# Moving quarter-array products of the recurrence beside others of their form in a two-layer decoder trunk

## The chip, the cores and the metric

The kernel runs on one core of a Trainium2 chip, as one program. The metric is the device time of one execution in microseconds (us). Lower is better. The engines are named as the profile names them: PE (TensorE, matrix products), PEld (its weight loads), DVE (VectorE), ACT (ScalarE), POOL (GpSimd) and SP (SyncE, which issues the DMAs).

## What is computed

Two layers, each with a parallel mix of heads and an MLP, on 512 positions of width 1024 in float32:

```python
for l in range(DEPTH):                       # 2
    h = rms_norm(x, norm_mix_g[l])
    proj = h @ w_in[l]                       # 1024 -> 26 groups of 128 columns
    p_att, p_conv, p_rwkv = jnp.split(proj, ...)
    o_att  = diff_attention(q, k, v, ...)    # 6 heads, two softmaxes each, causal
    o_conv = short_conv(...)
    o_rwkv = rwkv7_time_mix(p_rwkv, ...)     # 6 heads, a recurrence over 512 steps
    x = x + concat(o_att, o_conv, o_rwkv) @ w_out[l]
    h = rms_norm(x, norm_mlp_g[l])
    x = x + square(relu(h @ w_mlp_up[l])) @ w_mlp_down[l]
return rms_norm(x, final_norm_g)

# the recurrence in rwkv7_time_mix, for each head (state 64 x 64):
sa    = state @ (-kk_t)
state = state * w_t + sa (kk_t * a_t)^T + v_t k_t^T
y_t   = state @ r_t
```

## The kernel before

Large products (`pj` for the input projection, `po` for the output, `up`, `dn` and others for the MLP) are done in three passes of a split of both factors into a high and a low part; each pass is a 128x512 product on the whole array of PE. `raw` is a weight tile as it lands, `whi` and `wlo` its parts, `ahim` and `alom` those of the activations.

In the mix part of a layer other work is woven between these passes. The recurrence is done in chunks of 64 positions, two heads at a time: a *chain* t (0, 1, 2) for each pair of heads, written as `rwkv_pair(t)`, and the inverse that it needs, `rwkv_inverse(t)`. Their products are 64x64 blocks, so each uses a quarter of the array (64 rows by 64 columns of it) and four run on the quarters in turn. Groups that matter here, by their names in the profile: `pg` (the Gram products, two calls of `gram`, each into two banks of PSUM), `pbv` (16 products from `kq` and `vt`; ACT copies the result into `ab`), and in the inverse `px` and `py` (16 products each; ACT copies `px` into `rt`, which `py` needs), then `pz` and `pzz` on 32x32 blocks. `phsk` is a small product on columns of ones; DVE reads it into `rk`.

Attention (`att_pair`) is done row block by row block: `sc` (scores, two per block) on PE, a masked minimum `pp`/`mx` on DVE, two exponentials on ACT, three operations on DVE that end in `pp`, its transpose `ptt` on PE, a copy `pT` on ACT, and after four blocks the product `po<-v,pT`. `sc` and `ptt` share two banks.

What the order is, is written out by hand. Each of these functions is a generator that issues one instruction, or one group of products, and yields. `ORDER[l]` is a string with one letter for each step of a generator, and a count: `m` is the next product of the large ones, `R`, `S`, `T` a step of `rwkv_pair(0)`, `(1)`, `(2)`, `r`, `s`, `t` one of `rwkv_inverse`, `A`, `B`, `C` one of `att_pair`. `drive` goes through the string:

```python
    for run in order.split():
        for _ in range(int(run[1:] or 1)):
            if next(work[run[0]], True) is None:
                raise RuntimeError("a step before what it needs: " + run)
```

Each engine then does its instructions in that order, and waits on semaphores for what they need. `SLOTS[l]` deals buffers: for each tile in the order of its making a digit says which of the tag's buffers it takes. `ps/rp` deals the four PSUM banks that the recurrence's products rotate through; a product that takes a bank waits for the last reader of what lay there before.

Counted from 0, step 26 of a `rwkv_pair` is the first half of its Gram products, step 57 is `pbv`, steps 58 and 59 are the two copies on ACT from `pbv` into `ab`, step 10 is the first operation of DVE on `phsk`. Step 43 of a `rwkv_inverse` is `px`, 44 and 45 are the copies into `rt`, 46 is `py`.

Of the kernel before, what the change touches and what calls it, by code (L numbers as in the profile page):

```python
# [22 lines left out]
S = 512  # L23
# [3 lines left out]
C = 64  # L27
# [29 lines left out]
      "xyxyyxxxyyxxyyxyxxyxyyxyyyyyyxxxyyyxyxyyyyyyyxxxxxyyyyyyyyyyxyxyxxxxyyxxyy")  # L57

ORDER = (
# [43 lines left out]

SLOTS = (
         "cp/rk 010 "
         "cp/ro 010 "
         "cp/rr 10 "
         "cp/rsx 01201201 "
         "cp/ry 010 "
         "cp/ys 010 "  # L110
         "dp/dkhi 010 "
         "dp/dklo 010 "
         "dp/dm 010 "
         "dp/dn 010 "
# [18 lines left out]
         "mp/ty 010101010 "  # L133
         "ps/at 101010101010101010101010101010101010101010101010101010101010101010101010101010101010 "
         "ps/mm 01011101010001010101010101010101010101010 "
         "ps/rp 01233303103210321031230123012301230123231021302130213203131203102310202130123012301230123012301230101320312 "
         "wp/raw 01201201210210210210210210210210210210210210210210210210210210210210210210 "
         "wp/sq 101011010101010 "
         "wp/whi 01201201201201201201201201201201201201201201201201201201201201201201 "
# [29 lines left out]
         "mp/ty 010101010 "  # L169
         "ps/at 010101010101010101010101010101010101010101010101010101010101010101010101010101010101 "  # L170
         "ps/mm 01010100101010101010110101010101010101010101 "
         "ps/rp 10321032103210321023102310231023102021301230123012301230130231203131023012302130120312031203210303120132 "
         "wp/raw 12012012012012010210210210210210210210210210210210210210210210210210210210 "
         "wp/sq 101010101 "
         "wp/whi 01201201201201201201201201201201201201201201201201201201201201201201201201 "
# [1455 lines left out]
```

## Time and profile before

| what | us |
|---|---|
| time, median of 3 runs | 1241.3 |
| lowest, highest of the runs | 1240.41, 1241.66 |
| the profiled execution: time | 1239.57 |
| the profiled execution: span | 1237.8 |

The profile shows one execution. Its page gives busy times of each engine and the chain of work that ended last; the timeline lists instructions of an engine by their start, with their duration, and x32 is the number of records in the row (a float32 product of 64x64 makes two). All times in the text below are microseconds from the start of the span. The mix part of layer 0 lies at the start of the span up to about 250, that of layer 1 between about 620 and 870.

### The profile page before, as it was taken

The numbers are of one execution on the slowest core, as the hardware profiler recorded it, in microseconds if no ns is written. First come the engines' busy times: TensorE is split into PE (matmuls) and PEld (weight loads), VectorE is DVE, ScalarE is ACT, GpSimd is POOL, SyncE is SP. The second block draws the span as 40 slices with busy tenths as digits, with TensorE's granted clock in tenths as the row PEclk, the third lists the DMA queues.
The fourth block names the chain that finished last, engine by engine and source line by source line (L and its number), as shares of the span: only waits on it lengthen the run. The fifth ranks groups of instructions, "written<-read, shape, count | busy, mean of one in ns | idle before, by whom it ended". The sixth has DMA issues, their size and how long they took to land.

```text
span 1237.8 us, 25529 instructions
## 1 busy us (share of the span) xinstructions
PE 1226.2 (99%) x9716; PEld 1055.3 (85%) x9716; DVE 932.3 (75%) x1804; ACT 692.3 (56%) x1462; POOL 350.2 (28%) x449
## 2 busy tenths in 40 slices
PE   9999999999999999999999999999999999999997
PEld 6788788888999898989888887888889999999987
DVE  6787888869987676765666777887799867676753
ACT  6785655648455454544465657464675545454542
POOL 1263637331121111120035455464202211111111
PEclk9999999999999999999999999999999999999999
DMA  6523334142433333321235244232433333323121
GB/s 217 164 87 100 106 95 111 53 153 86 136 103 98 107 95 103 98 90 44 68 102 168 76 119 119 87 90 70 154 109 121 106 101 102 103 96 109 52 69 68
DMA packets 84698, 127.94 MB, mean 103 GB/s; under 512 B 21472, under 2 KB 25568, under 8 KB 84576
## 3 DMA queue, kind: packets, MB, share of 16 engines
q1 hardware_dynamic: 83568, 125.64, 33.0%
q8 instruction: 76, 1.25, 0.4%
q10 hardware_dynamic: 1008, 0.68, 0.2%
q14 instruction: 46, 0.38, 0.1%
HBM read 117.11 MB, written 9.18 MB: 102 GB/s over the span
## 4 chain that ended last, share of the span: by engine, by line
PE 94%; ACT 2%; DVE 2%; POOL 1%; DMA 1%; issue 1%; ACTq 0%; POOLq 0%; DVEq 0%
PE dn L282 25%; PE pj L282 21%; PE pa L282 13%; PE po L282 8%; PE pb L282 7%; PE dnF L282 4%; PE pc L282 3%; PE up L282 3%; PE sc L282 1%; PE ptt L287 1%; PE pg L282 1%; PE pyy L282 1%; DMA raw<-wts 1%; PE pzw L282 1%; PE pst L282 1%
## 5 line engine op out<-in xcount | busy, mean ns | idle before, releaser
L1394 POOL TENSOR_TENSOR ml<-m,mh 128x512 fp32r<-128x512 f32 x56 | 91.1, 1645 | 496.2 <-ACT mh L1393 337.6
L282 PE MATMUL dn<-mh,whi 128*128 128x512 f32 x448 | 175.5, 392 | 0.0
L282 PE MATMUL dn<-mh,wlo 128*128 128x512 f32 x448 | 175.2, 391 | 0.0
L282 PE MATMUL dn<-ml,whi 128*128 128x512 f32 x448 | 175.0, 391 | 0.0
L683 POOL TENSOR_TENSOR wlo<-raw,whi 128x512 fp32r<-128x512 f32 x84 | 111.5, 1328 | 206.0 <-ACT whi L671 170.6
L344 ACT CAST whi<-raw 128x512 fp32r<-128x512 f32 x126 | 77.9, 619 | 157.2 <-PE dn L282 147.7
L282 PE MATMUL pj<-ahim,whi 128*128 128x512 f32 x392 | 156.9, 400 | 0.4 <-DVE vf L1280 0.4
L282 PE MATMUL pj<-ahim,wlo 128*128 128x512 f32 x392 | 156.4, 399 | 0.0
L282 PE MATMUL pj<-alom,whi 128*128 128x512 f32 x392 | 156.0, 398 | 0.0
L1540 DVE TENSOR_TENSOR x<-dn,x 128x512 f32<-128x512 f32 x108 | 74.5, 690 | 88.7 <-PE dn L282 88.6
L671 ACT CAST whi<-raw 128x512 fp32r<-128x512 f32 x142 | 87.7, 617 | 78.0 <-PE pj L282 28.8
L1463 ACT CAST shi_p<-s 128x512 fp32r<-128x512 f32 x112 | 69.5, 621 | 78.5 <-PE pa L282 59.4
L345 DVE TENSOR_TENSOR wlo<-raw,whi 128x512 fp32r<-128x512 f32 x126 | 97.8, 778 | 7.1 <-ACT whi L344 6.8
L282 PEld LDWEIGHTS dn<-mh,wlo 128*128 128x128 f32 x448 | 84.2, 188 | 18.6
L282 PEld LDWEIGHTS dn<-ml,whi 128*128 128x128 f32 x448 | 84.2, 188 | 17.2
L282 PEld LDWEIGHTS dn<-mh,whi 128*128 128x128 f32 x448 | 84.1, 188 | 17.3
L282 PE MATMUL pa<-thi,shi_p 128*128 128x256 f32 x336 | 95.2, 283 | 0.0
L282 PE MATMUL pa<-tlo,shi_p 128*128 128x256 f32 x336 | 94.9, 282 | 0.0
L282 PE MATMUL pa<-thi,slo_p 128*128 128x256 f32 x336 | 94.1, 280 | 0.0
L1464 DVE TENSOR_TENSOR slo_p<-s,shi_p 128x512 fp32r<-128x512 f32 x112 | 77.7, 696 | 21.6 <-ACT shi_p L1463 18.8
L282 PEld LDWEIGHTS pj<-ahim,whi 128*128 128x128 f32 x392 | 73.9, 188 | 14.1 <-issue 0.8
L282 PEld LDWEIGHTS pj<-alom,whi 128*128 128x128 f32 x392 | 73.9, 188 | 14.0 <-issue 0.5
(417 smaller groups left out, 3248.6 us busy)
## 6 DMA issues: line engine op xcount, KB each, us to landing
raw<-wts SPq DMA_DIRECT2D x389, 256.0 KB, 2.6
qs<-dqhi SPq DMA_DIRECT2D x24, 128.0 KB, 3.3
ks<-dkhi SPq DMA_DIRECT2D x24, 128.0 KB, 3.6
x<-xT SPq DMA_DIRECT2D x8, 256.0 KB, 4.5
dqhi<-qhi SPq DMA_DIRECT2D x6, 256.0 KB, 3.5
dqlo<-qlo SPq DMA_DIRECT2D x6, 256.0 KB, 3.4
dkhi<-khi SPq DMA_DIRECT2D x6, 256.0 KB, 3.0
dklo<-klo SPq DMA_DIRECT2D x6, 256.0 KB, 3.5
```

The costliest lines, as they stand in the source:

```text
L282: ins = nc.tensor.matmul(*a, **k)
L287: ins = nc.tensor.transpose(*a, **k)
L344: act.copy(hi[:, :n], raw[:, :n])
L345: (pool if a and lean[0] else dve).tensor_tensor(lo[:, :n], raw[:, :n], hi[:, :n].bitcast(F32), ALU.subtract)
L671: yield act.copy(hi[:, k0:k1], raw[:, k0:k1])
L683: yield eng.tensor_tensor(lo[:, k0:k1], raw[:, k0:k1], hi[:, k0:k1].bitcast(F32), ALU.subtract)
L1394: (dve if i < 4 else pool).tensor_tensor(lo, m, hi.bitcast(F32), ALU.subtract)
L1463: act.copy(hi, src)
L1464: dve.tensor_tensor(lo, src, hi.bitcast(F32), ALU.subtract)
L1540: dve.tensor_tensor(x[j], pt, x[j], ALU.add)
```

## The change

Only the two tables are changed; what each step does is as before. Five groups of products move, which are numbered here for later:

1. layer 0, chain 0: `pbv` goes from between a `ptt` and a `po` to right behind chain 0's `px`, 17 us later; its two ACT copies go behind the two copies into `rt`.
2. layer 0, chain 1: `pbv` goes from behind a `po` to right behind chain 1's `px`, 2 us later. The ACT copies stay.
3. layer 1, chain 0: `pbv` goes from between two `pj` to right behind chain 0's `px`, 15 us later; the ACT copies as in 1.
4. layer 1, chain 1: `pbv` goes from between two `sc` to right behind chain 1's `py`, 13 us later; the ACT copies with it.
5. layer 1, chain 2: the first half of the Gram products goes from ahead of a `ptt` to right behind it, where the second half stands.

In layer 1 also step 10 of chain 2 (DVE on `phsk`) goes from behind chain 1's work on `py` to ahead of it. The banks of `ps/rp` are dealt anew for both layers: 58 of 107 digits differ in layer 0 and 54 of 104 in layer 1.

Pieces of the two tables (the strings are otherwise the same, but broken into lines at other places):

```diff
-  ... A2 r R3 m3 r A R r B3 r A R2 A h w r2 m2 ...
+  ... A2 r R3 m3 r A r B3 r A2 h w r2 m2 ...
-  ... y A2 m4 A r3 d m4 h S2 ...
+  ... y A2 m4 A r R r2 R2 d m4 h S2 ...
...
-  "ps/rp 10321032103210321023102310231023102021301230123012301230130231203131023012302130120312031203210303120132 "
+  "ps/rp 10321032103210321032103210321032103031201320132103210132320132013232103120312031021302021302130202310321 "
```

The first two pairs are move 1: `R` is taken out at the top (step 57, and below it `R2`, steps 58 and 59) and put behind `r` (step 43) and `r2` (44 and 45).

The instructions of PE at the old place of move 3, before:

```order
L282 MATMUL pj1_19_8499<-ahim1_6_7883,whi117_4_8455 128x512
L282 MATMUL pbv1_0_0_8594<-vt1_0_8389,kq1_0_8307 64x64 x2
L282 MATMUL pbv1_0_1_8595<-vt1_0_8389,kq1_0_8307 64x64 x2
...
L282 MATMUL pj1_19_8499<-alom1_6_7884,whi117_4_8455 128x512
L282 MATMUL pj1_19_8499<-ahim1_6_7883,wlo117_4_8465 128x512
L287 MATMUL ptt1_0_0_0_8622<-cst_77,pp1_0_0_0_0_8568 128x128
```

and now (a name is that of the tile with its layer, chain and numbers of making; line numbers are one higher):

```order
L283 MATMUL pj1_19_8499<-ahim1_6_7883,whi117_4_8455 128x512
L283 MATMUL pj1_19_8499<-alom1_6_7884,whi117_4_8455 128x512
L283 MATMUL pj1_19_8499<-ahim1_6_7883,wlo117_4_8465 128x512
L288 MATMUL ptt1_0_0_0_8602<-cst_77,pp1_0_0_0_0_8568 128x128
L283 MATMUL pj1_19_8499<-ahim1_7_7917,whi117_4_8455 128x512
```

Sixteen products less lie ahead of the transpose. At the new place of move 3, ACT before:

```order
L1180 COPY rt1_0_8817<-px1_0_0_8799 128x4x64
L1180 COPY rt1_0_8817<-px1_0_1_8800 128x4x64
L671 CAST whi102_0_8830<-raw102_0_8712 128x512
L1335 COPY pT1_0_0_8628<-ptt1_0_0_3_8820 128x512
L801 ACTIVATE dr1_1_8882<-pr1_1_8852,drv1_100 128x512
```

and now:

```order
L1181 COPY rt1_0_8815<-px1_0_0_8779 128x4x64
L1181 COPY rt1_0_8815<-px1_0_1_8780 128x4x64
L1025 COPY ab1_0_8387<-pbv1_0_0_8797 128x4x64
L1025 COPY ab1_0_8387<-pbv1_0_1_8798 128x4x64
L672 CAST whi102_0_8830<-raw102_0_8692 128x512
L1336 COPY pT1_0_0_8608<-ptt1_0_0_3_8820 128x512
```

The two copies stand ahead of a cast and of the attention's copy. DVE in layer 1 where `py` of chain 1 is read, before:

```order
L802 SCALAR_TENSOR_TENSOR zr2_1_9768<-pr2_1_9853,prm1_67,dr2_1_9885 128x512
L1188 TENSOR_TENSOR x16_1_1_9839<-py1_1_0_9920,x16_1_1_9839 128x4x64
L1188 TENSOR_TENSOR x16_1_1_9839<-py1_1_1_9921,x16_1_1_9839 128x4x64
L1190 STREAM_TRANSPOSE yj1_1_9948<-x16_1_1_9839 128x512
L909 TENSOR_SCALAR rk1_2_9973<-phsk1_2_9908 128x8
```

and now:

```order
L803 SCALAR_TENSOR_TENSOR zr2_1_9748<-pr2_1_9833,prm1_67,dr2_1_9865 128x512
L910 TENSOR_SCALAR rk1_2_9897<-phsk1_2_9888 128x8
L1189 TENSOR_TENSOR x16_1_1_9819<-py1_1_0_9902,x16_1_1_9819 128x4x64
L1189 TENSOR_TENSOR x16_1_1_9819<-py1_1_1_9903,x16_1_1_9819 128x4x64
L1191 STREAM_TRANSPOSE yj1_1_9950<-x16_1_1_9819 128x512
```

The read of `phsk` into `rk` stands ahead of the reads of `py`, whose second half now takes the bank of `phsk`.

More of the change, by code (lines that the diff above doesn't have):

```diff
@@ L135 @@
          "ps/mm 01011101010001010101010101010101010101010 "
-         "ps/rp 01233303103210321031230123012301230123231021302130213203131203102310202130123012301230123012301230101320312 "
+         "ps/rp 01233303103210321031203120312031203120201321032103210230123012301230101320312031203123012301320132020312301 "
          "wp/raw 01201201210210210210210210210210210210210210210210210210210210210210210210 "
```

87 rows, old and new, of the table ORDER are left out of this document.

## The prediction

> **What bounds the kernel now.** I read the page first (busy shares, chain of waits), then the timeline of TensorE (PE) around each of the five places that lose or gain quarter products, then the timelines of VectorE (DVE), ScalarE (ACT) and GpSimd (POOL) at the same times for what becomes ready when.
>
> ```profile
> span 1237.8 us, 25529 instructions
> PE 1226.2 (99%) x9716; PEld 1055.3 (85%) x9716; DVE 932.3 (75%) x1804; ACT 692.3 (56%) x1462; POOL 350.2 (28%) x449
> PE 94%; ACT 2%; DVE 2%; POOL 1%; DMA 1%; issue 1%; ACTq 0%; POOLq 0%; DVEq 0%
> ```
>
> PE is busy for 99% of the span and is 94% of the chain that ended last. So every nanosecond taken from PE would count, if PE were never late for a reason of its own. But ends of matmuls are modelled and overlap, so a short wait of PE does not show as idle time. I therefore use distances between starts, and compare them with the end of whatever the next product needs.
>
> **What a crossing into quarters costs.** The timeline of PE where chain 0 of layer 1 has its `pbv` (time of start, duration, what):
>
> ```profile
> 678.56 0.39 PE L282 MATMUL pj<-ahim,wlo 128*128 128x512 f32 x1
> 678.79 0.39 PE L282 MATMUL pj<-ahim,whi 128*128 128x512 f32 x1
> 679.11 0.69 PE L282 MATMUL pbv<-vt,kq 64*64 64x64 f32 x32
> 679.74 0.50 PE L282 MATMUL pj<-alom,whi 128*128 128x512 f32 x1
> 680.08 0.40 PE L282 MATMUL pj<-ahim,wlo 128*128 128x512 f32 x1
> 680.33 0.33 PE L287 MATMUL ptt<-cst,pp 128*128 128x128 f32 x1
> ```
>
> A `pj` follows a `pj` after 0.23 us (678.56 to 678.79), but `pbv` follows one after 0.32: entering costs 0.09. `pbv` holds PE until 679.74, 0.63 us. Standing alone it costs 0.72. The same group beside another of its form:
>
> ```profile
> 91.50 0.69 PE L282 MATMUL px<-yi,ee 64*64 64x64 f32 x32
> 92.12 0.50 PE L282 MATMUL pj<-ahim,whi 128*128 128x512 f32 x1
> ...
> 826.27 0.27 PE L282 MATMUL py<-x,rt 64*64 64x64 f32 x2
> 826.78 0.65 PE L282 MATMUL pbv<-vt,kq 64*64 64x64 f32 x32
> 827.36 0.34 PE L282 MATMUL po<-v,pT 128*64 128x64 f32 x4
> ```
>
> `px` alone takes 0.62 (91.50 to 92.12); `py` with `pbv` right behind takes 1.09 (826.27 to 827.36). The second group adds 0.47, which is 0.25 less than 0.72. For the Gram products of chain 2 in layer 1, apart, and those of chain 0 in the same layer, together:
>
> ```profile
> 659.72 2.12 PE L282 MATMUL pg<-ar,bk 64*64 64x128 f32 x80
> 661.77 0.50 PE L282 MATMUL pj<-alom,whi 128*128 128x512 f32 x1
> ...
> 788.20 1.24 PE L282 MATMUL pg<-ar,bk 64*64 64x128 f32 x48
> 789.37 0.66 PE L287 MATMUL ptt<-cst,pp 128*128 128x128 f32 x4
> 789.96 1.10 PE L282 MATMUL pg<-ar,bk 64*64 64x128 f32 x32
> 790.99 1.21 PE L282 MATMUL po<-v,pT 128*64 128x64 f32 x34
> ```
>
> The first half alone: 1.17 plus 0.09 for entering, 1.26. Together both take 2.05, the second alone 1.03: beside it the first adds 1.02, so 0.24 is saved. In all 4 x 0.25 + 0.24 = 1.24 us, 0.10% of the time. This is all that the change can give on PE. [...]
>
> **What the old places did.** A group that is taken out frees 0.72 (1.26 for the Gram half) only if the next products are ready earlier. What released them:
>
> ```profile
> 74.42 0.85 PE L282 MATMUL pbv<-vt,kq 64*64 64x64 f32 x32
> ...
> 81.45 0.09 POOL L798 MEMSET pk<- 128x1 f32 x1
> 81.60 1.75 DVE L802 SCALAR_TENSOR_TENSOR zk<-pk,prm,dk 128x512 f32<-128x512 f32 x1
> 86.22 0.48 DVE L1326 SCALAR_TENSOR_TENSOR pp<-sc,sm,pp 128x256 f32<-128x256 f32 x1
> 86.86 0.38 PE L287 MATMUL ptt<-cst,pp 128*128 128x128 f32 x2
> 87.28 0.37 ACT L1335 COPY pT<-ptt 128x256 f32<-128x256 f32 x1
> 87.70 0.44 PE L282 MATMUL sc<-ks,qs 96*128 96x384 f32 x1
> ...
> 154.36 0.33 PE L282 MATMUL py<-x,rt 64*64 64x64 f32 x4 [0.40 <-ACT rt L1180]
> ...
> 679.92 0.35 DVE L1326 SCALAR_TENSOR_TENSOR pp<-sc,sm,pp 128x128 f32<-128x128 f32 x1
> ...
> 750.10 0.37 ACT L1335 COPY pT<-ptt 128x256 f32<-128x256 f32 x1 [0.67 <-PE ptt L287]
> 751.02 0.44 PE L282 MATMUL sc<-ks,qs 96*128 96x384 f32 x1
> 751.12 0.65 ACT L1024 COPY ab<-pbv 128x256 f32<-128x256 f32 x2
> ...
> 788.26 0.75 DVE L1326 SCALAR_TENSOR_TENSOR pp<-sc,sm,pp 128x512 f32<-128x512 f32 x1
> ```
>
> Move 3 (layer 1, chain 0) is the plainest. The softmax row ends at 679.92 + 0.35 = 680.27 and `ptt`, its transpose, starts at 680.33: 0.06 later, the hand-over itself. Without `pbv` PE stands there at 679.61 and waits for DVE. Freed: 0, not 0.72. At the new place beside `px` it adds 0.47. Net +0.47.
>
> Move 1 (layer 0, chain 0): `pbv` leaves 74.42, and PE comes early until the `ptt` of 86.86. Its softmax row ends at 86.22 + 0.48 = 86.70. It stands behind `zk`, which waits for the POOL memset of 81.45, behind the inverse on POOL, and that doesn't move. So 0.10 could be gained, but the next `sc` at 87.70 waits for the copy `pT`, which ends at 87.28 + 0.37 = 87.65; ACT takes it when the cast before it lets go. Freed: 0. New place: +0.47.
>
> Move 2 (layer 0, chain 1): old and new place lie before the `py` of 154.36, for which PE waits 0.40 for ACT as it is. What is freed is lost there, and the 0.47 added behind `px` fall into the same wait. Net 0.
>
> Move 4 (layer 1, chain 1): `pbv` stands between two `sc`; the second needs the bank that the copy `pT` frees at 750.47, so with the 0.06 of a hand-over it can start at 750.53 instead of 751.02. Freed: 0.49, of the 0.72. Added: 0.47. Net 0 without the bank below.
>
> Move 5 (Gram half): the softmax row ends at 788.26 + 0.75 = 789.01; `ptt` could start at 789.07 instead of 789.37. Freed: 0.30 of 1.26. Added behind `ptt`: 1.02. Net +0.72.
>
> [...]
>
> **The banks.** The new deal gives some tiles of the pairs a bank whose last reader is later. I followed each tile of the four rotating banks to its last reader, and two wait:
>
> ```profile
> 224.34 0.37 ACT L1024 COPY ab<-pbv 128x256 f32<-128x256 f32 x1
> 224.48 0.22 PE L282 MATMUL pzz<-xs,rt 32*32 32x32 f32 x2
> ...
> 762.12 0.75 DVE L1326 SCALAR_TENSOR_TENSOR pp<-sc,sm,pp 128x512 f32<-128x512 f32 x1
> 762.78 0.74 DVE L802 SCALAR_TENSOR_TENSOR zr<-pr,prm,dr 128x512 f32<-128x512 f32 x1
> 763.25 0.27 PE L282 MATMUL py<-xs,rt 64*64 64x64 f32 x2
> 765.32 0.13 DVE L909 TENSOR_SCALAR rk<-phsk 128x8 f32<-128x8 f32 x1
> ```
>
> In layer 0 the second half of chain 2's `pzz` (224.48) now takes the bank of `pbv`, whose first half ACT copies until 224.34 + 0.37 = 224.71; with 0.06 that is 224.77: +0.29. In layer 1 the second half of chain 1's `py` (763.25) takes the bank of `phsk`. Its reader `rk` is moved ahead on DVE for that, behind `zr`, but `zr` ends at 763.52; the 0.13 of `rk` and 0.06 make 763.71 at most, 0.46 late, and some 0.08 less if DVE's rows overlap as `pp` and `zr` do (762.12 + 0.75 = 762.87 against 762.78): +0.38.
>
> **Copies on ACT.** The two copies of `ab` go with moves 1, 3 and 4, behind the copies of `px` (0.65 us for both where they stand now in layer 1, 751.12). On ACT everything behind comes up to 0.65 later, and `pzz` waits for ACT. Bounds 0 and 3 x 0.65 = 1.95; ACT is idle for 44% of the span, so I stay near the lower end: +0.1. No DMA is issued by a moved step. POOL's queue keeps its order, and its `nm` of chain 2, behind move 5's half, comes later by some 0.7 into an inverse that I take to have that much room.
>
> **The sum.** 0.47 + 0 + 0.47 + 0 + 0.72 + 0.29 + 0.38 + 0.1 = +2.4 us. The profiled execution took 1239.57 (1237.8 of span and 1.8 around it) and would take 1242.0. It is 1.7 below the median of 1241.3; so 1243.7 for the median, 0.19% more. From no change a measurement of this kernel tells about 0.2%, 2.5 us; the forecast lies just inside.
>
> **Rivals.**
> 1. *The crossings are saved and nothing waits.* If the softmax rows end earlier too when PE is earlier, each move keeps its 0.25: -1.24, and with the banks' waits absorbed 1240.1. For it: DVE takes `sc` from PE, so its chain follows PE in part. Against: the released rows at 679.92 and 788.26 hang on ACT's exponentials, and `zk` on POOL. [...] It decides where the rows named end 0.3 us or more before PE's arrival.
> 2. *Half and half.* The waits of moves 3 and 1 stay, but the Gram half and the banks cost nothing: 0.47 + 0.47 + 0 = +0.9, 1242.2, no change that can be told.
> 3. *ACT becomes the bound behind the moved copies.* `pzz` comes 0.65 late in each of moves 1, 3 and 4: +1.95 instead of 0.1, so +4.3, 1245.6. For it: `xs`, `rt` and `pT` stand right behind on ACT. Against: ACT has gaps. It decides when ACT has no gap of 0.65 between `px` and `pzz`.
> 4. *The order isn't what decides* (no wait, no saving): 1241.3. Against: the `ptt` of 680.33 comes 0.06 behind its row, so taking 0.72 from in front of it can't pass unseen.
>
> **Numbers.** Forecast (waits where the filler stood): 0.62, its own range 1242.4 to 1245.0, of which 0.28 lies over 1243.8. Rival 1: 0.15; 0.04 of it lies over 0.2% faster, if waits of before vanish with it. Rival 2: 0.12. Rival 3: 0.09. Rival 4: 0.02. Faster 0.04, slower 0.28 + 0.09 = 0.37, within 0.2% the rest, 0.59. The range leaves out the lower half of rival 1 and the upper half of rival 3: 1240.1 to 1245.3.
>
> **What would show it.** Right: in the profile after, `ptt` of layer 1's first softmax starts 0.06 behind DVE's `pp` with PE waiting some 0.6 to 0.7; `px` and `pbv` take 1.09 together; both Gram halves take 2.05; `pzz` and `py` wait for `ab` and `rk`. Wrong: `ptt` starts without a wait, or `pp` ends earlier by what PE gained; then rival 1. If `pzz` waits for ACT's `rt` in moves 1, 3 and 4, rival 3.

## The result, and the profile after

| | changed kernel | before, same chip |
|---|---|---|
| median, us | 1245.65 (6 executions, 1242.42 to 1247.92) | 1239.99 (6, 1238.95 to 1241.66) |
| ratio | 1.0044 [1.0033, 1.0055] | |
| profiled execution, us | 1247.92, span 1246.1 | 1239.57, span 1237.8 |

The change costs 5.7 us, 0.44%. The forecast was +2.4 with 1245.3 as its upper end: too low. That forecast was counted from 1241.3, the median of the first three executions; counted from 1239.99 its upper end is +4.0, and the miss is larger. The page of the changed kernel (span; busy times; chain of waits; the queue of kind instruction):

```profile
span 1246.1 us, 25533 instructions
PE 1228.8 (99%) x9716; PEld 1057.4 (85%) x9716; DVE 934.3 (75%) x1804; ACT 692.1 (56%) x1462; POOL 349.6 (28%) x449
PE 91%; DVE 3%; ACT 2%; DMA 2%; POOL 1%; issue 1%; ACTq 0%; POOLq 0%; DVEq 0%
q8 instruction: 76, 1.25, 0.4%
```

PE's share of the chain that ended last fell from 94% to 91%; DVE and DMA have 3% and 2%. That is a wait of PE for DVE, and of DVE for a DMA. I looked for it by the start of the same product in both traces, which gives the growth of PE's delay from place to place:

| place (us in before) | forecast | profiled execution of the changed kernel |
|---|---|---|
| start to 72 | 0 | -0.30 |
| move 1 | 0.47 | +0.55 |
| move 2 | 0 | 0.00 |
| bank of `pzz`, layer 0 | 0.29 | +0.28 |
| move 3 | 0.47 | +0.68 |
| move 4 and the bank of `py`, 749.5 to 785 | 0.38 | **+5.83** |
| move 5 | 0.72 | +0.71 |
| rest, to 1234 | 0.1 | +0.33 |

The start differs from one execution to the next without any change there (-0.96 in two experiments below). All but one of the other places are near the forecast. At moves 1, 3 and 5 the softmax rows did not come earlier; the timeline of PE there:

```profile
86.54 0.44 PE L288 MATMUL ptt<-cst,pp 128*128 128x128 f32 x2 [0.53 <-DVE pp L1327]
...
91.24 0.69 PE L283 MATMUL px<-yi,ee 64*64 64x64 f32 x32
91.75 0.65 PE L283 MATMUL pbv<-vt,kq 64*64 64x64 f32 x32
...
679.90 0.39 PE L283 MATMUL pj<-ahim,wlo 128*128 128x512 f32 x1
681.13 0.33 PE L288 MATMUL ptt<-cst,pp 128*128 128x128 f32 x1 [0.84 <-DVE pp L1327]
...
694.96 0.69 PE L283 MATMUL px<-yi,ee 64*64 64x64 f32 x32
695.47 0.65 PE L283 MATMUL pbv<-vt,kq 64*64 64x64 f32 x32
696.05 0.66 PE L288 MATMUL ptt<-cst,pp 128*128 128x128 f32 x4
...
796.24 0.66 PE L288 MATMUL ptt<-cst,pp 128*128 128x128 f32 x4 [0.80 <-DVE pp L1327]
796.83 2.12 PE L283 MATMUL pg<-ar,bk 64*64 64x128 f32 x80
798.88 0.80 PE L283 MATMUL po<-v,pT 128*64 128x64 f32 x20
```

Each `ptt` waits 0.53 to 0.84 for its row, `px` with `pbv` takes 1.09 (694.96 to 696.05), both Gram halves 2.05 (796.83 to 798.88): these steps ran as the prediction says. The place that did not is the `px` of chain 1, on PE and on DVE:

```profile
762.32 0.39 PE L283 MATMUL pj<-ahim,wlo 128*128 128x512 f32 x1
765.99 1.13 PE L283 MATMUL px<-yi,ee 64*64 64x64 f32 x32 [3.27 <-DVE yi L1173]
767.05 1.02 PE L283 MATMUL phsk<-cst,ksq 128*64 128x2 f32 x16
...
771.67 0.63 PE L283 MATMUL pj<-alom,whi 128*128 128x512 f32 x1
```

```profile
758.63 0.08 DVE L1313 DVE_READ_ACCUMULATOR2_ANT mx<- 128x1 f32 x1
760.95 1.18 DVE L1154 TENSOR_TENSOR x<-xd,cst 128x512 f32<-128x512 f32 x1 [2.25 <-DMA xd<-dm]
762.16 1.83 DVE L1162 TENSOR_TENSOR xs<-xd,cst 64x256 f32<-64x256 f32 x2
764.02 0.69 DVE L798 TENSOR_TENSOR pr<-pj,rsm 128x512 f32<-128x512 f32 x1
764.63 0.68 DVE L1171 TENSOR_TENSOR ee<-nn,cst 128x512 f32<-128x512 f32 x1
765.23 0.70 DVE L1173 STREAM_TRANSPOSE yi<-x 128x512 f32<-128x512 f32 x1
```

The same rows of DVE in the kernel before:

```profile
757.71 0.09 DVE L1312 DVE_READ_ACCUMULATOR2_ANT mx<- 128x1 f32 x1
757.71 0.69 DVE L1153 TENSOR_TENSOR x<-xd,cst 128x512 f32<-128x512 f32 x1
758.43 0.85 DVE L1161 TENSOR_TENSOR xs<-xd,cst 64x256 f32<-64x256 f32 x2
...
759.92 1.22 DVE L1170 TENSOR_TENSOR ee<-nn,cst 128x512 f32<-128x512 f32 x1
761.07 0.70 DVE L1172 STREAM_TRANSPOSE yi<-x 128x512 f32<-128x512 f32 x1
```

and of PE:

```profile
761.44 0.39 PE L282 MATMUL pj<-ahim,wlo 128*128 128x512 f32 x1
761.82 0.69 PE L282 MATMUL px<-yi,ee 64*64 64x64 f32 x32
```

Before, DVE takes `xd` (a block that the inverse sends through memory, `dm` out and `xd` in) directly behind `mx`, without a wait, and `px` at 761.82 finds `yi` just done (761.07 + 0.70 = 761.77). That leaves 0.05 of room from `yi` to `px`. After, DVE stands 2.25 for `xd`, runs beside POOL's casts of weight tiles (`x` 1.18 instead of 0.69, `xs` 1.83 instead of 0.85), and `px` waits 3.27. POOL after:

```profile
760.30 1.29 POOL L684 TENSOR_TENSOR wlo<-raw,whi 128x512 fp32r<-128x512 f32 x1 [3.97 <-ACT whi L672]
762.37 1.35 POOL L684 TENSOR_TENSOR wlo<-raw,whi 128x512 fp32r<-128x512 f32 x1 [0.78 <-ACT whi L672]
```

Then PE itself is slow: `px` takes 1.13 instead of 0.69, a `pj` 0.63 instead of 0.39. The view by windows (us, then busy time with count of PE, PEld, DVE, ACT and POOL, granted clock of PE, DMA share, GB/s):

```profile
762.00:765.00 3.00, 0.71 (x4) 0.25 (x2) 2.92 (x5) 0.54 (x2) 1.43 (x3) 1.00 0.33 109
765.60:772.30 6.70, 6.32 (x120) 5.31 (x122) 4.07 (x12) 2.57 (x7) 0.00 (x0) 0.50 0.02 7
```

The granted clock is 1.00 while PE waits and 0.50 from 765.55 to 772.38, 6.83 us. So the +5.83 are: -0.46 freed between the two `sc` (0.49 was forecast); +3.29 at `px` (the last `pj` ahead of it is 0.88 later than before, 762.32 against 761.44, and `px` 4.17); the 0.47 of `pbv`'s new place; what is left, some 2.5, goes with the 6.83 us at half clock. The wait of `py` for `rk` isn't there: `rk` is done at 768.28, and at half clock the first half of `py` keeps PE until 768.43.

The larger part of why `xd` is late is in the DMA view of the transfer's time, issue to landing (queue: packets, MB, share of 16 engines; then the issues with the time to landing). The changed kernel, 757.0 to 760.9:

```profile
q1 hardware_dynamic: 1292, 0.54, 60.0%
q8 instruction: 1, 0.02, 1.9%
...
xd<-dm SPq DMA_DIRECT2D x1, 64.0 KB, 3.9
```

The kernel before, 755.0 to 757.2:

```profile
q1 hardware_dynamic: 1081, 0.15, 45.1%
...
xd<-dm SPq DMA_DIRECT2D x1, 64.0 KB, 2.2
```

A packet of the queue q8 lies in the transfer now; before, there was none. PE issues 9716 matmuls and 9716 weight loads, 19,432 instructions; over the 76 packets of q8 that is 256 a packet. From this count I take the packets to be PE's own instructions; each has 16 KB. `pbv` is 32 matmuls and 32 loads, a quarter of a packet. Taken out of the stream ahead, it lets the next packet be asked for 64 instructions later, that is 32 passes of `pj` with their loads, by an estimate 7.4 us at 0.23 each: the packet that came at 751.8 before comes at 758.6, 6.8 later and 1.59 behind the issue of `xd`. It occupies one of the 16 DMA engines for 1.2 us (1.9% of 16 x 3.9). Fifteen of the sixteen parts of `xd` land 2.0 to 2.3 us after the issue, the last one after 3.93.

The packet is not all of it. `x` starts 3.24 later than before (760.95 against 757.71) where PE is 0.88 late, so 2.36 of it is lateness: 1.72 from the landing (3.93 against 2.21) and 1.12 from the issue (2.00 later, 757.00 against 755.00), less the 0.50 for which `xd` lay ready before. Of the 1.12, 0.46 is what move 4 freed for PE but not for the inverse (ahead of move 4 PE was 1.34 late, and `nb`, the inverse's first transfer, was issued 1.39 later), and 0.38 is that `nb` landed in 2.65 instead of 2.27, with a packet of q8 0.63 behind its issue. The two casts of POOL add 0.49 at `x` and 0.98 at `xs`, and `ee`, which no longer runs beside one, gives back 0.54: 2.36 + 0.49 + 0.98 - 0.54 = 3.29, the whole growth at `px`.

### The profile page after: what moved, and what is told of

Read it like the earlier page. It is cut to its first block, busy times and chain, and to the rows that moved or that the text cites. A ratio compares the mean times of both kernels' runs of the same rounds, so it can differ in the third digit from the quotient of the medians.

```text
span 1246.1 us, 25533 instructions
## 1 busy us (share of the span) xinstructions
PE 1228.8 (99%) x9716; PEld 1057.4 (85%) x9716; DVE 934.3 (75%) x1804; ACT 692.1 (56%) x1462; POOL 349.6 (28%) x449
## 3 DMA queue, kind: packets, MB, share of 16 engines
q8 instruction: 76, 1.25, 0.4%
## 4 chain that ended last, share of the span: by engine, by line
PE 91%; DVE 3%; ACT 2%; DMA 2%; POOL 1%; issue 1%; ACTq 0%; POOLq 0%; DVEq 0%
PE dn L283 25%; PE pj L283 19%; PE pa L283 13%; PE po L283 8%; PE pb L283 7%; PE dnF L283 4%; PE pc L283 3%; PE up L283 3%; PE sc L283 1%; PE ptt L288 1%; DMA raw<-wts 1%; PE pg L283 1%; PE pyy L283 1%; PE pzw L283 1%; PE pst L283 1%
```

## The experiments

The thirteen runs at a glance (median of n executions against the median before on the same chip; the wait of `px` of chain 1 and the length at half clock between 764 and 778, both in the profiled execution; how many executions had a mean clock of 0.996 or less, of which the kernel before had 0 in 91; a single 3.41 us at half clock can still read 0.997, as in the profiled execution of e7_late2):

| run | what | median (n) | before | ratio [95%] | `px` waits | half clock | clock <= 0.996 |
|---|---|---|---|---|---|---|---|
| the change | | 1245.65 (6) | 1239.99 | 1.0044 [1.0033, 1.0055] | 3.27 | 6.83 | 4 of 6 |
| e5_again | the same kernel | 1244.83 (4) | 1239.64 | 1.0044 [1.0028, 1.0060] | 3.21 | 3.41 | 2 of 4 |
| e1_only4 | move 4 alone | 1240.44 (12) | 1239.83 | 1.0015 [1.0005, 1.0025] | 0 | 0 | 3 of 12 |
| e2_no4 | all but move 4 | 1242.61 (9) | 1239.83 | 1.0025 [1.0016, 1.0034] | 0 | 0 | 0 of 9 |
| e4_early | a cast moved from POOL to DVE | 1242.47 (11) | 1239.83 | 1.0023 [1.0014, 1.0032] | 0 | 0 | 0 of 11 |
| e3_cover | six `pj` put into the wait | 1246.18 (5) | 1239.83 | 1.0050 [1.0038, 1.0062] | 0 | 3.41 | 5 of 5 |
| e6_ahead | `pbv` ahead of `px` | 1243.48 (5) | 1239.64 | 1.0039 [1.0026, 1.0051] | 0 | 0 | 1 of 5 |
| e7_late2 | before, `yi` 2 products later | 1244.89 (4) | 1239.64 | 1.0043 [1.0030, 1.0057] | 2.88 | 3.41 | 2 of 4 |
| e8_late4 | before, `yi` 4 products later | 1245.28 (4) | 1239.64 | 1.0045 [1.0030, 1.0060] | 4.29 | 10.24 | 4 of 4 |
| e9_border | the change, +64 PE instructions at the start | 1242.59 (11) | 1239.96 | 1.0019 [1.0010, 1.0028] | 0.21 | 0 | 0 of 11 |
| e10_hit | before, packets shifted | 1239.98 (10) | 1239.96 | 0.9999 [0.9990, 1.0008] | 0 | 0 | 0 of 10 |
| e11_hit126 | the same, other shift | 1241.19 (10) | 1239.75 | 1.0011 [1.0000, 1.0022] | 0 | 0 | 3 of 10 |
| e12_hit130 | the same, other shift | 1240.42 (10) | 1239.75 | 1.0001 [0.9992, 1.0011] | 0 | 0 | 1 of 10 |
| e13_hit122 | the same, other shift | 1241.54 (11) | 1239.55 | 1.0013 [1.0004, 1.0022] | 1.70 | 0 | 1 of 11 |

**Which move is it? e1_only4, e2_no4.** Pieces of the order of layer 1; e1_only4, e2_no4 and e6_ahead also deal three to six banks otherwise, so that the order can run. First, before with move 4 alone:

```diff
-  ... s2 B m B2 S s w S2 s ...  m2 B2 T2 s T3 s5 B m2 B s3 B T10 ...
+  ... s2 B m B2 s w s2 B2 ...  m2 B2 T2 s T4 s3 S3 s2 B m2 B s3 B T9 ...
```

> The kernel before with move 4 alone (pbv of chain 1 in layer 1 taken from between two sc and put behind py, its copies and the rk step with it, banks of these three products as in the changed kernel). Theory L (the inverse of chain 1 in layer 1 comes late: POOL, then the transfer xd, then DVE; px waits some 3 us, and PE gets half its clock for some 8 us behind that wait), in two forms. L4, the trigger is move 4 itself: px waits about 3 us and the granted clock falls; +4 to +5 us over before. L-shift, the trigger is the delay that moves 1 to 3 bring before the inverse: here px waits only the 0.49 us that pbv leaves free, on top of the 0.15 of before; with 0.47 at the new place and 0.1 to 0.4 for the bank +0.7 to +1.4 us, full clock. Rival S (the long wait of px is an accident of the one profiled execution; the 5.5 us are spread over the five moves): about +1 us, full clock.

+0.6, and `px` (761.50) waits for nothing; `py` waits 0.41 for `rk`. The packet arrives outside the transfer (3.38 behind the issue of `xd`, which lands in 2.28), since the delays of moves 1 and 3 aren't there. But three of twelve executions came at 1244.5 to 1245.9 with a mean clock of 0.994 or 0.995.

The changed kernel with the left side of that piece put back:

> The changed kernel without move 4 (moves 1, 2, 3 and 5 stay; pbv of chain 1 in layer 1, its copies and the rk step of chain 2 back where they were). Theory L4: px waits under 0.5 us, full clock, +2 us over before (0.47 + 0 + 0.47 + 0.72 + 0.29). L-shift: POOL's inverse is late as in the changed kernel, px waits some 2.5 to 3 us, the clock falls behind it, +4 to +5.5 us. Rival S: four fifths of it, about +4.5 us, with px waiting under 0.5 us and full clock.

+2.8. `px` does not wait, the packet is back at 752.2 and no execution has a mean clock of 0.996 or less. So by the medians neither half alone makes the loss: move 4 makes it on top of the others' delay. Three slow executions of move 4 alone remain, of which no profile was taken. By place this run reads +0.51 at move 1, -0.01 at move 2, +0.28 at the `pzz` bank, +0.52 at move 3, +0.72 at move 5, +0.27 in the rest: every term of the forecast by itself.

**Is it the late row ahead of `px`? e4_early, e3_cover, e6_ahead.** The first half of one cast (piece 118 of the weights) goes from POOL, where it delays the inverse, to DVE; the changed kernel otherwise:

```diff
-  LO, piece 118: first half "y"     ORDER: ... y ...
+  LO, piece 118: first half "x"     ORDER: ... x ...
```

> The changed kernel with one weight cast of layer 1 (wlo of 118, first half, 1.29 us), which stands between the steps of chain 1's inverse on POOL, done by DVE instead, at the same place in the order. Theory L: POOL's inverse ends 1.3 us or more earlier, dm and xd are issued that much earlier, px waits under 2 us, the clock holds: +2.4 to +3.5 us over before. If it is not POOL that sets xd, or the transfer itself was the accident: px waits some 3 us as before, +5.5. Rival S: no change against the changed kernel, +5.5.

`xd` is issued at 755.2 instead of 757.0, the packet comes 2.99 us behind that, and `xd` lands in 2.55. PE in this run:

```profile
761.75 0.69 PE L283 MATMUL px<-yi,ee 64*64 64x64 f32 x32
...
763.69 0.27 PE L283 MATMUL py<-xs,rt 64*64 64x64 f32 x2 [0.41 <-DVE rk L910]
```

No wait at `px`, no half clock; the place costs +0.61 and the whole +2.6. The wait of `py` for `rk`, of which the forecast spoke, appears with 0.41. This shows that the loss hangs on `xd` and the row behind it, not on the moved products. It doesn't part the late issue from the packet, since both are gone here.

Next the wait was filled from behind, with six passes of `pj`, six `m` from behind put ahead of `px`:

```diff
-  ... m2 B2 T2 s T4 s3 S3 s2 B m2 B s3 B T9 ...
+  ... m2 B2 T2 m6 s T4 s3 S3 s2 B2 s3 B T9 s B ...
```

> The changed kernel with six passes of pj (those that stand behind py and ptt of chain 1 in layer 1, 6 x 0.227 us) moved ahead of px, so that PE has 1.36 us more work while DVE is late. Theory L: the wait of px falls from 3.3 to about 1.9 us; if the granted clock then holds, 1.4 + 2 us are saved, less up to 0.5 for the six passes missing as filler later: +2.3 to +3 us over before, 2.5 to 3 under the changed kernel; if it falls all the same, +4.5. Rival S: no change against the changed kernel within 0.5 us, +5.5.

+6.3: missed. `px` doesn't wait, but the passes did not cover a late `xd`: in this execution the packet came 2.46 behind the issue, and `xd` landed in 2.35. Instead `pzz` waits, since the passes that stood in its own gap have been used up; and the clock falls there. PE and the windows view of this run:

```profile
771.66 0.49 PE L283 MATMUL pzz<-x,rt 32*32 32x32 f32 x3 [1.04 <-ACT rt L1208]
...
773.28 2.58 PE L283 MATMUL pzw<-ab,x 64*64 64x128 f32 x32
```

```profile
773.90:777.20 3.30, 3.30 (x34) 2.78 (x35) 2.43 (x7) 2.65 (x13) 1.43 (x2) 0.50 0.45 164
```

In the third, `pbv` stands directly ahead of `px` and so takes 0.5 of the wait; its copies go with it:

```diff
-  ... T2 s T4 s3 S3 s2 B m2 ...
+  ... T2 S3 s T4 s5 B m2 ...
```

> The changed kernel, but pbv of chain 1 in layer 1 (move 4) stands directly ahead of px instead of behind py, its two copies with it: still beside a group of its form, but in front of the product that waits for DVE. Theory L+filler (move 4 costs because PE comes 0.49 us earlier to a px that is not ready): px waits as in before (0.2 us), the group adds no wait, 0.25 us of crossing are saved; +2.1 to +2.4 us over before and full clock in all executions. Rival (the trigger is the delay of moves 1 and 3 or the new banks): +4 to +5.5 us, clock 0.996 or less.

+3.8, missed too. `xd` isn't late here (2.33; the packet comes 3.4 behind the issue), so the wait to be filled wasn't there. Instead the two copies of `ab` stand ahead of `ksq` on ACT, and `phsk` waits for it:

```profile
764.72 0.63 PE L283 MATMUL phsk<-cst,ksq 128*64 128x2 f32 x16 [0.89 <-ACT ksq L905]
```

**The same kernel again, e5_again.**

> The changed kernel once more, for a second profiled execution of it. Theory L+clock (the wait of px is long in most executions, by varying amounts, and the clock falls behind it): px waits 1.3 us or more, half clock for 3.3 or 6.8 us behind it, +5.5 us over before, and most of the listed mean clocks are 0.996 or less. Rival (the profiled execution was an accident, the extra time lies elsewhere): px waits about 0.4 us as in the runs with the early inverse, and the lost time shows at another place.

The wait is there again (3.21; `xd` in 3.90, its packet at 1.73), with one stretch of 3.41 us at half clock instead of two. Over both runs of the changed kernel seven of ten executions lie at 1245.1 to 1247.9; three, at 1242.4 to 1243.1, lie where the terms of the forecast end. The loss is thus not in each execution. None of those three was profiled, so that no packet falls into their `xd` is inferred.

**What does a late `yi` alone cost? e7_late2, e8_late4.** The kernel before, with two or four idle products on DVE ahead of the row, written into `x16` and overwritten:

```diff
+  for _ in range(2 if n == "1_1" else 0):      # 4 in e8_late4
+      dve.tensor_tensor(x16, nn, m16.unsqueeze(1).to_broadcast([P, N8, C]), ALU.mult)
```

> The kernel before, with two further DVE products of 128x512 (0.6 us each, into x16, which is written anew behind them) ahead of x16 of chain 1 in layer 1, so that px comes 1.2 us later and PE stands for about 1.4 us. Theory C (a gap of about 1.5 us beside quarter products is enough to halve the granted clock): +1.2 us for the wait and 1.2 to 2.5 us more in most executions, mean clock 0.996 or less there. Rival C0 (the clock falls only behind gaps of 3 us or more): +1.2 us, clock 0.997 to 0.998.

> As the run before, with four such products: px 2.4 us later, PE stands for about 2.6 us. Theory C: +2.4 us for the wait and 1.2 to 3.5 us more, in nearly all executions, mean clock 0.994 to 0.996. Rival C0: +2.4 us in all, clock 0.997 to 0.998.

PE in the two runs:

```profile
765.79 0.69 PE L282 MATMUL px<-yi,ee 64*64 64x64 f32 x32 [2.88 <-DVE yi L1172]
```

```profile
767.05 1.13 PE L282 MATMUL px<-yi,ee 64*64 64x64 f32 x32 [4.29 <-DVE yi L1172]
```

Two products, 1.4 us of DVE, make a wait of 2.88, since both `xs` now run beside POOL's cast (2.82 for the pair instead of 0.85; `ee` behind them gains back 0.54: 1.41 + 1.97 - 0.54 = 2.84). And both runs lose clock, 3.41 and 10.24 us of it, with nothing of the change in them. In the profiled executions the clock costs about 1.0 us (late2) and 2.9 (late4) beyond the wait, by an estimate from two starts: `px` comes 3.97 and 5.23 later than before, the first `pg` of chain 2 (793.18 and 796.28 against 788.20) 4.98 and 8.08. So a late `yi` alone can bring both the wait and the loss of clock.

**Is it the packet? e9_border, e10 to e13.** The strongest test leaves every product of the change where it is and shifts the borders of the packets. The kernel starts with idle products on PE; 42 of 64x64 instead of 10 of 128x512 are 64 more instructions, which is what `pbv` took away:

```diff
-  for _ in range(10): pe.matmul(idle, zero[:, :P], zero, ...)
+  for _ in range(42): pe.matmul(idle[:64, :64], zero[:, :64], zero[:, :64], ...)
```

> The changed kernel with 42 warm-up products of 64x64 at the start instead of 10 of 128x512, so that PE has 64 instructions more ahead of all its work; the order of the work is unchanged. PE's instructions come in packets of 16 KB (256 of them), so every such packet is fetched 64 instructions of work earlier; 64 is what pbv of move 4 counts. Theory F (the fetch at 758.6 us, which in the kernel before comes at 751.8, holds up the last sixteenth of xd): the packet comes at 751 to 752, all of xd lands within 2.7 us, px waits under 0.7 us, the clock holds (0.997 or more in all executions); +2.8 us over before, give or take 0.7 for the other start. Rival (where the packets lie doesn't matter; the order of work makes px late): px waits some 3 us, +5.5.

+2.6, and 11 of 11 executions between 1241.3 and 1243.8. The packet comes at 753.3, ahead of `xd`. DMA view 756.66 to 759.4 (no packet of q8) and PE in this run:

```profile
q1 hardware_dynamic: 1167, 0.31, 49.3%
...
xd<-dm SPq DMA_DIRECT2D x1, 64.0 KB, 2.7
```

```profile
763.35 0.69 PE L283 MATMUL px<-yi,ee 64*64 64x64 f32 x32 [0.21 <-DVE yi L1173]
...
765.28 0.27 PE L283 MATMUL py<-xs,rt 64*64 64x64 f32 x2 [0.41 <-DVE rk L910]
```

3 us are gone though not one product of the change was undone. The 0.21 of `px` is a little too good: in this execution a weight tile landed late for the softmax row near 684, PE came to `px` 0.44 later than in the changed kernel, and `px` waits about so much less. The time is not flattered by that, since the late row itself cost 0.57. The reverse was tried on the kernel before, with 117, 126, 130 and 122 idle products of 32x32 so that a packet would fall into its `xd`:

```diff
-  for _ in range(10): pe.matmul(idle, zero[:, :P], zero, ...)
+  for _ in range(117): pe.matmul(idle[:32, :32], zero[:, :32], zero[:, :32], ...)   # 126, 130, 122
```

> The kernel before, its order unchanged, with 117 warm-up products of 32x32 at the start instead of 10 of 128x512: 214 instructions more, which in steps of 256 puts each fetch 42 instructions of work later; the one at 751.8 us comes at about 756.6, 1.6 us behind the issue of xd. Theory F: the last sixteenth of xd lands 3.5 to 4 us after its issue instead of 2.2, x16 starts some 1.2 us later, px waits 1 to 3 us, the clock is halved behind it in some executions; +2 to +5 us on top of what the longer start costs (estimate 1 to 4 us from 117 pairs at 0.06 us against 3.7 us). Rival: only the start costs, px waits 0.15 us as before.

> As the run before (the order of the kernel before, more warm-up products of 32x32 at the start), with 126 of them instead of 117. At 117 the packet of instructions came at 758.0 us, 3.55 us behind the issue of xd and so behind its landing, and the longer start cost nothing. 18 instructions more ahead of the work are 9 passes of pj, 2.0 us: the packet should come at 756.0, 1.5 us behind the issue. Theory F: the last sixteenth of xd lands 3.3 to 4 us after its issue, x16 starts 0.5 to 1.2 us later than with 117 products, and px waits 0.7 us or more; with no more than that the clock holds: +0.5 to +2 us over before, more in executions in which the clock falls. Rival (a packet beside xd does not hold it up): xd lands in 2.2 us, +0.

> The same with 130 warm-up products: 8 instructions, 0.9 us more, the packet at about 755.1, 0.6 us behind the issue of xd. Theory F: the packet holds up one sixteenth of xd from its start; it lands 2.5 to 3.5 us after its issue, less late than with 126 products; +0 to +1.2 us. Rival: xd lands in 2.2 us, +0.

> The order of the kernel before, with 122 warm-up products of 32x32 at the start. The packet of instructions came at 758.0 us with 117 of them and at 755.65 with 126, in both outside the stretch from some 0.5 to 2 us behind the issue of xd (3.55 and 0.02 us). With 122 it should come between 756.5 and 757, 1.2 to 1.9 us behind the issue. Theory F: the last sixteenth of xd lands 3.3 to 4 us after its issue, x16 starts 0.5 to 1.5 us later than in the kernel before, px waits 0.6 us or more, and in some executions the clock falls (0.996 or less): +0.8 to +3 us over before. Rival: xd lands in 2.2 to 2.7 us whatever the packet does, px waits under 0.3 us, +0, and no clock under 0.997.

The first three missed the window. e10: the packet came 3.53 behind the issue, behind the landing; 1239.98 shows that the other start costs nothing. e12: at 752.0, ahead of `dm`; no change. e11: 0.02 behind the issue, `xd` in 2.25, no wait in the profiled execution; but three of its ten executions had a mean clock of 0.994 to 0.996, and the cause of that stays open. e13 hit, 0.72 behind the issue. DMA view 754.3 to 757.8, DVE and PE:

```profile
q8 instruction: 1, 0.02, 2.5%
...
xd<-dm SPq DMA_DIRECT2D x1, 64.0 KB, 3.4
```

```profile
757.80 0.69 DVE L1153 TENSOR_TENSOR x<-xd,cst 128x512 f32<-128x512 f32 x1 [0.50 <-DMA xd<-dm]
758.52 1.86 DVE L1161 TENSOR_TENSOR xs<-xd,cst 64x256 f32<-64x256 f32 x2
```

```profile
763.03 0.69 PE L282 MATMUL px<-yi,ee 64*64 64x64 f32 x32 [1.70 <-DVE yi L1172]
```

With the order of before, one packet makes `xd` land in 3.4, DVE wait 0.50, `xs` run beside POOL (1.86 for the pair instead of 0.85), and `px` wait 1.70; PE's delay against before grows by 1.71 there and nowhere else. This is the chain of the changed kernel, made without it. The clock held in the profiled execution (1.00 from 763 to 776).

## Why the prediction was wrong

**The step that failed** is the line of move 4, "Net 0 without the bank below", with the sentence "No DMA is issued by a moved step" in *Copies on ACT*. That sentence is true of SP's queue. But a moved product takes its own instructions along, and these come by DMA: by the count above 256 in each of the 76 packets of q8, of which one came at 758.6 instead of 751.8, and `xd`, a transfer of 64 KB, took 3.9 us beside it instead of 2.2. For move 4 the working followed what waits behind the old and the new place; it never asked what PE fetches meanwhile, nor whether `px` of chain 1, which stands between the two places, had room for a later `xd`. It had next to none: 761.77 against 761.82. The one inverse that the prediction took "to have that much room" is chain 2's, and that one had it: its `px` waits for nothing after the change. I had quoted `zr` and `py` from just behind the place and not the row ahead of `px`. The loss there is 3.3 of wait and some 2.5 of clock in the profiled execution, and the 3.0 between the medians of the change and of e9_border.

**The sum.** Where the packet does not hit, the terms hold:

| term | forecast | the change | e9_border | e4_early | e2_no4 |
|---|---|---|---|---|---|
| move 1 | 0.47 | 0.55 | 0.26 | 0.50 | 0.51 |
| move 2 | 0 | 0.00 | -0.01 | 0 | -0.01 |
| bank of `pzz` | 0.29 | 0.28 | 0.27 | 0.27 | 0.28 |
| move 3 | 0.47 | 0.68 | 1.17 | 0.55 | 0.52 |
| move 4, bank of `py` | 0.38 | 5.83 | 0.80 | 0.61 | 0.09 |
| move 5 | 0.72 | 0.71 | 0.71 | 0.72 | 0.72 |
| rest | 0.1 | 0.33 | 0.71 | 0.30 | 0.27 |

(e2_no4 has no move 4. Of the 1.17 of e9_border 0.57 is a softmax row that came later near 684, behind a weight tile that landed late, as in e1_only4, e7_late2 and e8_late4, which lack move 3, and in e3_cover; of its 0.71, 0.39 lies at the very end.) The medians of e9_border and e4_early are 2.6 above before, the three low executions of the change 2.4 to 3.4, against the 2.4 of the sum. So move 1, 3 and 5's reading, that what is taken out from ahead of a released row frees nothing, is right, with 0.53 to 0.84 of new wait in front of each `ptt`; and so are the two banks.

**Mis-sized terms.** Copies on ACT: 0.1 forecast, 0.3 measured, and not by ACT. In the rest `zv` on DVE took 1.66 where POOL's cast had begun 0.18 ahead of it, instead of 0.76 where it began 0.18 behind, and chain 2's `ptt` and `pz` came 0.13 and 0.17 later. Move 4: net 0 forecast, +0.2 to +0.4 in the runs without a hit (0.61 and 0.80 less the bank's 0.41).

**The rivals.** Rival 1 (saved crossings, 1240.1) fell: every `ptt` waits. Rival 2 (+0.9) fell: the Gram half cost 0.71 and the banks 0.28 and 0.41. Rival 4 fell with the waits. Rival 3's 1245.6 is the measured time by luck, since its mechanism isn't there: `pzz` waits for `rt` only in e3_cover, where I took its cover away. A range that ends at the forecast's mechanisms was too narrow for a place with no room.

**What stays open.** Why three of ten executions of the change escape: no profile of one was taken. Why e11_hit126 and e1_only4 have three executions each at a lower clock, though their profiled ones show no wait at `px`: in e11 a packet 0.7 later would lie where that of e13_hit122 did (+0.02 against +0.72 behind the issue), in e1 it lay 1.1 us behind the landing of `xd` (3.38 against 2.28), and none of the six was profiled. Whether a version with the borders of e9_border and the 1.24 us of the crossings exists wasn't tried; the waits in front of `ptt` speak against it.

## What to carry to other kernels

Moving a product moves its instructions too: count them (a 64x64 product in float32 is two matmuls and two loads here), and look which short transfer on the critical path the next packet of instructions will fall into; a profile shows the packets in the queue of kind instruction. Before a move is costed at nothing, look at the row *ahead* of the next product that waits for another engine: here it ended 0.05 us before PE arrived, and a late transfer became a wait of 3.27 with 6.83 us at half clock behind it. Borders can be shifted by idle instructions at the start (64 more put the packet of 758.6 at 753.3), which is a test for this cause. Here it was a cure too (1245.65 to 1242.59), but it shifts all 76 packets, and e13_hit122 shows the same means doing harm.

## What the runs showed of the hardware

**A packet of PE's instructions delayed the last part of a small transfer.** `nb` and `xd` are 64 KB in over a thousand packets. In layer 1, chain 1, they landed in 2.0 to 2.7 us when no packet of q8 began within them. With one that began 0.6 to 1.7 us behind the issue they took 2.65 to 3.93: `nb` +0.62 to 2.71, +0.91 to 3.21, +1.25 to 3.24; `xd` +0.72 to 3.40, +1.59 to 3.93, +1.73 to 3.90. One right at the issue of `xd` (+0.02, e11_hit126) did no harm there, 2.25. Elsewhere it did: `xd` of layer 1's chain 2 took 2.94 to 3.94 in the ten profiles that have a packet of q8 between 0.47 ahead of its issue and 0.59 behind it, and 2.46 to 2.79 in the five that have none there. The kernel before is among the ten (3.31), and nothing waits, since that `px` has room (`yi` is done at 824.34, `px` starts at 824.83): here the room decided and not the packet alone.

**The clock.** The stretches at half clock between 764 and 778 are 3.41, 6.83 or 10.24 us long, one, two or three times 3.41. The length of PE's wait alone does not tell whether one follows: behind waits of 2.88 (e7_late2) and of 1.04 among 32x32 products (e3_cover) the granted clock was 0.50, behind 1.70 after whole passes (e13_hit122) it was 1.00. And in the changed kernel a second 3.41 us stayed at half clock though PE was busy for 6.32 of 6.70 us, mostly with quarter products.

What the half clock goes with can be estimated from the traces, with 3.41 us taken as the length of a window. In the five profiles with a stretch at half clock between 764 and 778, that stretch begins a whole number of windows (136 to 139) ahead of the one at the end of the span, so I take the end to fix the grid of windows in every profile. For each window I add up the columns that its products stream (512 for a pass, 64 for each record of a 64x64 product, a product across a border by its share in time). A window full of passes has some 7,700 (3.41 / 0.227 x 512). Of 5309 windows in 15 profiles, without those at the start and the end of the span, the eight that half clock follows have 1134 to 3287; of all others one has less than 3600 (3495, e7_late2). So, by this estimate, the clock in these 15 profiles went by how much PE streamed in a fixed window and not by the length of a gap: the 1.70 of e13_hit122 lies in a window with 4073, the 1.04 of e3_cover in one with 3228.

**DVE beside POOL.** The same `xs` took 0.42 alone and 1.39 to 1.42 beside POOL's cast (e5_again, e7_late2, e13_hit122); POOL's `tt` of 15 columns took 0.21 in a gap of DVE (before, 735.43) and 0.77 beside it (the changed kernel, 737.20). The second `xs` of the changed kernel ends 0.27 behind POOL's cast (763.99 against 763.72). What holds the one up beside the other is not shown. In e7_late2, where the delay pushed both `xs` into POOL's time, it grew on the way: 1.4 us put in, 2.88 out.
